# Other PSUM banks for a transposed output, and work moved between slots, in a hybrid SGU and GLA block

## The chip, the cores and the metric

One core of one Trainium2 chip runs the whole layer as a single launch. TensorE (PE) multiplies, VectorE (DVE), ScalarE (ACT) and GpSimd (POOL) do the rest, and SyncE (SP) issues the DMAs. The metric is device time in microseconds, from runs of the whole program; lower is better. All numbers of the profile come from one execution, taken by the hardware profiler.

## The reference, cut to what matters

The layer takes x, 512 tokens of 1024 channels in float32, and computes

```
p   = x @ W_in + b_in        # u, v | q, k, vg, r, low-rank gate | g_A, g_B
y_A = gelu(u) * (W_s layernorm(gelu(v)) + b_s)   # per 128-token chunk, 8 groups, W_s lower triangular
y_B = rmsnorm(gla(q, k, vg, gate)) * gn * silu(r)   # 4 heads, decay per key channel
m   = sigmoid(g_A) * y_A + sigmoid(g_B) * y_B
h   = layernorm(alpha * x + m @ W_out)
out = layernorm(alpha * h + relu(h @ W_1)^2 @ W_2)   # inner width 4096
```

The gated linear attention (gla) is causal: token t sees token s at or before it with the weight q_t k_s exp(sum of the log gates between them), summed over 128 key channels of a head.

## The kernel before, in words

**Products.** Every large product is made three times: both operands are split into a high half (a cast on ScalarE, L90) and a low half (a subtraction on VectorE, L91), and high x high, high x low and low x high are added up in one PSUM bank. A group is 24 matmuls (8 slices of the inner dimension, three passes) into one bank. The four banks of `ps_m` take the groups in turn; `ps_a` has two more single banks (tag `aux`) for everything small; `ps_s` holds one tile of two banks for the attention scores (tag `sc`).

**Weights.** They come as 146 chunks of 128x1024, in the order that `_stream` (L1019) writes out. `load_to` (L102) issues a chunk's DMA on SP into a raw buffer, `split_to` (L127) makes its two halves in the next of the seven buffers of `wpool`, so chunk i + 7 is split as soon as PE is done with chunk i. The last matrix product needs eight chunks at once; the eighth, the very last, is put aside into a part of `xh` and `xl` that is free by then (L135).

**Slots.** `pump` (L183) runs behind each group of the first part and gives out, in the order in which they were planned, the small jobs that `at` has put on that slot. The groups are: V in slots 0 to 7 (L634), U in 8 to 15 (L649), Q and K of the second head pair in 16 to 19 (L674), the values VG in 20 to 27 (L697), g_A in 28 to 35 (L704), then r, r, g_B, g_B four times from slot 36 on (L734, L769).

**Scores.** For each of two pairs of heads, `plan_pair` (L530) takes a list of 20 steps, counted from slot 0 for the first pair and from 16 for the second: the gates; for each of three levels a difference (`level_diff`), the exponent and products (`level_prep`) and the scores of the two heads (`level_score`, L474); the diagonal (`diag_prep`, `diag_score`) of the two heads; the part between chunks (`inter`); two transposes (`kd_turn`, L393). The exponents of the keys, `kt`, have one buffer, so a level's `kt` waits for the scores of the level before. The scores' tile has one buffer too. `chunk_out` (L499) makes one chunk's output of one head in an `aux` bank, from slot 29 on for the first pair and 35 on for the second.

**The gating unit.** `mix` (L652) multiplies one channel group by its W_s into an `aux` bank, and VectorE reads it (L658) and multiplies it into u (L666). Two of them stand in the hand-over of each Q or K group of slots 16 to 19 (L678).

**Branches.** `r_take` (L709) transposes the normalised output of the attention into an `aux` bank, `yt`, and multiplies it with silu(r) (L714).

**The order of the engines.** PE runs in the order in which the program is written. The other engines' order is set by a planner that works with its own costs, up to line 803; from there on (the two layers of width 4096) ScalarE, VectorE and GpSimd run in program order too.

**The two layers.** The inner width is cut into four blocks of 1024. For three of them the second layer is done with seven products in place of eight (Strassen's scheme): `seven_products` (L879) yields the products P0 to P6, in the order `ORDER`, each with two chunks of weights (some of them sums or differences of two loaded chunks, L124) and an operand that is made one product ahead (`operand`, L847: a difference L824, a high half, a low half). Between them lie eight pieces j0 to j7 of the first layer for the next block, each a group with one chunk (`block`, L834): j0 P0 j1 P1 ... j5 P5 j6 j7 P6. The chunks in the stream stand in the same order. After P4 and P5 of the last block, `together` (L905) adds partial results up on VectorE, three and four operations. Then both halves of the last block are split in parts (`in_parts`, L942: `Fs` behind P5, `xh` and `xl` ahead of P6), and the last matrix product (L972 on) runs over eight chunks: four with `Fs`, four with `xh`.

Of the kernel before, what the change touches and what calls it, by code (L numbers as in the profile page):

```python
# [8 lines left out]
F32 = mybir.dt.float32  # L9
# [6 lines left out]
P = 128  # L16
# [4 lines left out]
KT = D // P  # L21
DK = 128
DV = 256
NCH = T // P
# [25 lines left out]
def hybrid_block(  # L50
# [23 lines left out]
    def pool(stack, name, **kw):  # L74
        kw.setdefault("bufs", 1)
        return stack.enter_context(tc.tile_pool(name=name, reuse_waits="tile", **kw))
# [9 lines left out]
    ps_s = pool(ctx, "ps_s", bufs=1, space=PSUM)  # L86
    ps_a = pool(ctx, "ps_a", bufs=2, space=PSUM)
# [6 lines left out]
    NB = DF // 512  # L94
    STREAM = _stream()
    NCHUNK = len(STREAM)

    raws, chunks, kept = {}, {}, {}
    lanes, ring = {0: rpool}, {lane: [] for lane in LANES}
# [2 lines left out]
    def load_to(n):  # L102
        while state["load"] < min(n, NCHUNK):
            i = state["load"]
            kind, lane, key, news = STREAM[i]
            if news is not None:
                ends = ring[lane]
                if len(ends) >= LANES[lane] and ends[-LANES[lane]] >= state["split"]:
                    break
                raw = lanes[lane].tile([P, 1024], F32, name=f"raw{i}", tag="raw")  # L110
                nc.sync.dma_start(raw, w_all[news])
                kept.setdefault(key, []).append(raw)
                users = [j for j in range(i + 1, NCHUNK) if STREAM[j][2] == key]
                users = [j for n_, j in enumerate(users) if all(STREAM[x][3] is None for x in users[:n_])]
                ends.append(max([i] + (users if key else [])))
            raws[i] = kept[key][-1:] if kind == "one" else kept[key][-2:]
            state["load"] = i + 1

    def sum_to(n):
        while state["sum"] < min(n, state["load"]):  # L120
            i = state["sum"]
            raw, *other = raws[i]
            if other:
                nc.vector.tensor_tensor(raw, raw, other[0], op=ALU.add if STREAM[i][0] == "sum" else ALU.subtract)  # L124
            state["sum"] = i + 1

    def split_to(n):  # L127
        while state["split"] < min(n, NCHUNK):
            i = state["split"]
            load_to(i + 1)  # L130
            if i < NCHUNK - 1:
                hi = wpool.tile([P, 1024], F32R, name=f"wh{i}", tag="wh")
                lo = wpool.tile([P, 1024], F32R, name=f"wl{i}", tag="wl")
            else:
                hi, lo = (a[:, 4:6, :].rearrange("p k t -> p (k t)") for a in (xh, xl))  # L135
            sum_to(i + 2)
            raw = raws[i][0]
            if i:
                split(hi, lo, raw)
            chunks[i] = (hi, lo)  # L140
            state["split"] = i + 1
        load_to(n + sum(LANES.values()) if 1 in lanes else n + RAW_BUFS)
# [381 lines left out]
    pr0 = pair_new(0, gp0)  # L524
# [5 lines left out]
    def plan_pair(pr, n0, steps):  # L530

        at(n0 + steps[0], lambda: gates(pr))
        for lv in range(3):
            d_, p_, s0, s1 = steps[1 + 4 * lv : 5 + 4 * lv]
            at(n0 + d_, lambda lv=lv: level_diff(pr, lv))
            at(n0 + p_, lambda lv=lv: level_prep(pr, lv))
            at(n0 + s0, lambda lv=lv: level_score(pr, lv, 0))
            at(n0 + s1, lambda lv=lv: level_score(pr, lv, 1))
        p0, p1, s0, s1, i_, k0, k1 = steps[13:]
        for j, (p_, s_) in enumerate(((p0, s0), (p1, s1))):  # L540
            at(n0 + p_, lambda j=j: diag_prep(pr, j))
            at(n0 + s_, lambda j=j: diag_score(pr, j))
        at(n0 + i_, lambda: inter(pr))
        at(n0 + k0, lambda: kd_turn(pr, 0))
        at(n0 + k1, lambda: kd_turn(pr, 1))

    S_V, S_U, S_QK = 0, 8, 16
    S_VG, S_GA = 20, 28
    S_R, S_O = 36, 52
    plan_pair(pr0, 0, (1, 3, 3, 5, 6, 7, 7, 8, 10, 11, 11, 12, 13, 13, 14, 14, 16, 16, 17, 18))  # L550


    def ln_apply(dst, src, st, g, b, tmpp, tag, parts=1):
# [57 lines left out]
    def col_job(name, take):  # L611
        u0 = take_chunks(1)
        col_group(xh, xl, u0, name, slice(0, T), take)
        pump()
        split_to(u0 + 1 + W_BUFS)
# [4 lines left out]
    def u_take(e):  # L620
        return lambda ps: nc.scalar.activation(AT_[:, e, :], ps, AF.Gelu_apprx_tanh, bias=col("u", e))
# [24 lines left out]

    at(S_U + 1, mix_bias)

    for e in range(KT):  # L649
        col_job(f"u{e}", u_take(e))  # L650

    def mix(g):  # L652
        gs = slice(g * P, (g + 1) * P)
        pm = ps_a.tile([P, NCH, P], F32, name=f"pm{g}", tag="aux")
        for c in range(NCH):
            nc.tensor.matmul(pm[:, c, :], bufB[:, c, gs], wst[:, g, :], start=True, stop=True)
        tm = temp(f"mx{g}")
        nc.vector.scalar_tensor_tensor(  # L658
            tm.rearrange("p (c s) -> p c s", s=P),
            pm,  # L660
            col("sgg", g),
            mixb[:, gs].unsqueeze(1).broadcast_to([P, NCH, P]),
            op0=ALU.mult,
            op1=ALU.add,
        )
        nc.vector.tensor_mul(AT_[:, g, :], AT_[:, g, :], tm)  # L666


    pr1 = Pair()
    pr1.hp = 1  # L670
    pr1.q = gt.tile([P, 2, T], F32, name="q1", tag="q")
    pr1.k = gt.tile([P, 2, T], F32, name="k1", tag="k")
    plan_pair(pr1, S_QK, (2, 4, 5, 6, 7, 7, 8, 9, 10, 10, 10, 12, 13, 13, 15, 15, 16, 16, 17, 18))
    for e in range(4):  # L674

        def take(ps, e=e):
            qk_take(pr1, e, ps)
            mix(2 * e)  # L678
            mix(2 * e + 1)

        col_job(f"qk1_{e}", take)
    sgu.close()
# [24 lines left out]

    def r_take(e, t1):
        def f(ps):  # L709
            pt = ps_a.tile([P, NCH, P], F32, name=f"yt{e}", tag="aux")  # L710
            for c in range(NCH):
                nc.tensor.transpose(pt[:, c, :], bufB[:, c, e * P : (e + 1) * P], ident)
            nc.scalar.activation(t1, ps, AF.Silu, bias=col("r", e))
            nc.vector.scalar_tensor_tensor(  # L714
                t1.rearrange("p (c s) -> p c s", s=P),
                pt,
                col("gn", e),
                t1.rearrange("p (c s) -> p c s", s=P),
                op0=ALU.mult,
                op1=ALU.mult,  # L720
            )

        return f
# [203 lines left out]
    for p in range(PAIRS - 1):  # L927
        F_ = fp.tile([P, 2, 4, T], F32, name=f"F{p + 1}", tag="F")
        jobs = block(take_raw(F_, 0)) + block(take_raw(F_, 1))
        for n, product in enumerate(seven_products(F, p, F_)):  # L930
            jobs[n]()
            if n == 6:
                jobs[7]()
            product()
        F = F_

# [2 lines left out]
    jobs = block(take_raw(F_, 0)) + block(take_raw(F_, 1))  # L939
# [6 lines left out]
        return hi, lo  # L946

    for n, product in enumerate(seven_products(F, PAIRS - 1, None)):
        jobs[n]()
        if n == 6:  # L950
            jobs[7]()
            parts.append(in_parts(1, hh[:, 0:4, :], hl[:, 0:4, :]))
        product()
        if ORDER[n] == 4:
            together(7, ((1, 4),))
            together(4, ((1, 2),), (1, 0))
        if ORDER[n] == 1:
            together(6, ((1, 1), (-1, 2), (1, 3)))
            together(7, ((1, 1),))
        if n == 5:  # L960
            Fs = fp.tile([P, 2, 4, T], F32R, name="Fs", tag="F")
            parts.append(in_parts(0, Fs[:, 0], Fs[:, 1]))
    split_to(NCHUNK)
    together(7, ((-1, 5),))
# [54 lines left out]
def _stream():  # L1019

    n = 16 * 4
    out = [("one", 0, None, c) for c in range(n)]
    f1 = n
    f2 = n + 4 * (DF // 512)
    f1_jobs = iter(range(f1, f2))
    take = lambda k: [("one", 0, None, next(f1_jobs)) for _ in range(k)]

    def operand(p, m, h):  # L1030
        b = lambda i, j: f2 + 8 * p + 2 * (2 * (i - 1) + j - 1) + h
        kind, c = {
            2: ("one", b(1, 1)),
            6: ("sum", b(1, 2)),
            3: ("sum", b(2, 2)),
            5: ("one", None),
            7: ("sum", b(2, 1)),
            4: ("sum", b(1, 1)),
            1: ("less", b(2, 2)),
        }[m]  # L1040
        return (kind, h, (p, h), c)

    out += take(8)
    for p in range(PAIRS):
        products = [[operand(p, m, h) for h in range(2)] for m in ORDER]
        for i, product in enumerate(products):
            out += take(1 + (i == 6)) + product
    out += [("one", 0, None, f2 + 8 * PAIRS + c) for c in range(8 * (DF // 1024 - PAIRS))]
    return out

# [73 lines left out]
```

## Time and profile before

| | |
|---|---|
| median of 3 runs | 780.04 us (779.6 to 780.37) |
| the profiled execution | 780.24 us, its span 778.3 us |
| PE | 758.2 us busy, 97% |
| VectorE | 489.9 us, 63% |
| ScalarE | 355.5 us, 46% |
| GpSimd | 67.3 us, 9% |
| HBM traffic | 82.48 MB read, 2.10 MB written |

In the rows of the profile the first number of a timeline row is the start, the second the duration, both in us; [2.14 <-DVE qt L437] is idle time of the engine just before and what ended it. A row of the waits has the total, the number of times and the longest. A row of the chain has start, duration, engine, tile, line and how many instructions are merged. A matmul's end is modelled, so neighbours overlap in the rows.

### The profile page before, as it was taken

Reading aid. Unit: us, or ns where it says so; the run is one execution under the profiler, and the core shown is the slowest. Engines: PE = TensorE matmul, PEld = TensorE weight load, DVE = VectorE, ACT = ScalarE, POOL = GpSimd, SP = SyncE. Lnnn points to the kernel's source line nnn. Section 1 sums busy time; section 2 is a strip of 40 time slices with the busy share of each in tenths; the row PEclk is TensorE's granted clock in tenths of the full one; section 3 lists DMA queues with packets and bytes.
Section 4 is the critical chain, followed back from the end, with each engine's and each line's share of the span. In section 5 each row is a group of like instructions: output and inputs, shape, how many; then the busy total and the mean of one; then the engine's idle time right before and its main releaser. Section 6 shows DMA issues by size and latency. Waiting matters only on the chain.

```text
span 778.3 us, 8853 instructions
## 1 busy us (share of the span) xinstructions
PE 758.2 (97%) x3498; PEld 629.6 (81%) x3498; DVE 489.9 (63%) x584; ACT 355.5 (46%) x453; POOL 67.3 (9%) x87
## 2 busy tenths in 40 slices
PE   9998999989999989999999999999999999999996
PEld 7887888877888877888888987888888888888785
DVE  6569756668666532445447545774687568769955
ACT  5476864354146444454322444555554445454300
POOL 1015400013202211000001000000000000000011
PEclk9999999999999999999999999999999999999999
DMA  8723332200341231422232422444144424335111
GB/s 275 267 79 105 111 120 81 82 28 28 108 136 55 101 116 32 135 92 88 101 99 78 163 82 83 160 136 136 56 161 136 149 69 151 128 126 163 54 55 54
DMA packets 25609, 85.15 MB, mean 109 GB/s; under 512 B 3104, under 2 KB 3360, under 8 KB 25568
## 3 DMA queue, kind: packets, MB, share of 16 engines
q1 hardware_dynamic: 25568, 84.59, 33.1%
q8 instruction: 27, 0.44, 0.2%
q14 instruction: 14, 0.11, 0.1%
HBM read 82.48 MB, written 2.10 MB: 109 GB/s over the span
## 4 chain that ended last, share of the span: by engine, by line
PE 85%; DVE 6%; ACT 3%; issue 2%; POOL 1%; DMA 1%; SPq 0%; DVEq 0%; POOLq 0%; ACTq 0%
PE f L608 22%; PE m L898 14%; PE ps L204 12%; PE r L608 6%; PE gb L608 6%; PE u L608 6%; PE f L984 5%; PE ga L608 4%; PE first L271 2%; PE qk L608 2%; PE sc L478 2%; DVE wl L91 2%; DMA raw<-in_w_all 1%; POOL qt L419 1%; ACT wh L90 1%
## 5 line engine op out<-in xcount | busy, mean ns | idle before, releaser
L91 DVE TENSOR_TENSOR wl<-raw,wh 128x1024 fp32r<-128x1024 f32 x144 | 176.6, 1236 | 154.5 <-ACT wh L90 147.7
L90 ACT CAST wh<-raw 128x1024 fp32r<-128x1024 f32 x144 | 148.6, 1044 | 139.0 <-PE ps L204 34.0
L608 PE MATMUL f<-xh,wl 128*128 128x512 f32 (+1 forms) x288 | 105.5, 366 | 0.0
L608 PE MATMUL f<-xh,wh 128*128 128x512 f32 (+1 forms) x288 | 105.4, 366 | 0.0
L608 PE MATMUL f<-xl,wh 128*128 128x512 f32 (+1 forms) x288 | 105.4, 366 | 0.0
L898 PE MATMUL m<-wh,ol 128*128 128x512 f32 x168 | 66.5, 396 | 0.5 <-DVE ol L91 0.5
L898 PE MATMUL m<-wh,oh 128*128 128x512 f32 x168 | 66.6, 396 | 0.3 <-ACT oh L90 0.3
L898 PE MATMUL m<-wl,oh 128*128 128x512 f32 x168 | 66.3, 395 | 0.0
L608 PEld LDWEIGHTS f<-xl,wh 128*128 128x128 f32 x288 | 54.3, 189 | 9.0
L608 PEld LDWEIGHTS f<-xh,wh 128*128 128x128 f32 x288 | 54.3, 189 | 8.9
L608 PEld LDWEIGHTS f<-xh,wl 128*128 128x128 f32 x288 | 54.3, 189 | 8.8
L204 PE MATMUL ps<-wh,xh 128*128 128x512 f32 x128 | 51.1, 399 | 0.0
L204 PE MATMUL ps<-wl,xh 128*128 128x512 f32 x128 | 50.1, 391 | 0.0
L204 PE MATMUL ps<-wh,xl 128*128 128x512 f32 x128 | 50.0, 390 | 0.0
L827 ACT ACTIVATE F<-f 128x512 f32<-128x512 f32 (+1 forms) x28 | 15.0, 536 | 75.5 <-PE f L608 75.5
L124 DVE TENSOR_TENSOR raw<-raw,raw 128x1024 f32<-128x1024 f32 x30 | 36.6, 1221 | 7.3 <-DMA raw<-in_w_all 7.0
L419 POOL TENSOR_TENSOR qt<-cum 128x768 f32<-128x768 f32 (+2 forms) x18 | 30.3, 1713 | 115.5 <-DVE cum L374 102.2
L898 PEld LDWEIGHTS m<-wh,ol 128*128 128x128 f32 x168 | 31.6, 188 | 8.4 <-DVE ol L91 1.0
L898 PEld LDWEIGHTS m<-wh,oh 128*128 128x128 f32 x168 | 31.6, 188 | 7.9 <-ACT oh L90 0.7
L898 PEld LDWEIGHTS m<-wl,oh 128*128 128x128 f32 x168 | 31.7, 189 | 7.3
L991 POOL TENSOR_TENSOR rs_l<-rs_l,nhalf 128x1 f32<-128x1 f32 x4 | 3.9, 987 | 334.1 <-DVE rs_l L990 334.1
L90 ACT CAST oh<-d 128x1024 fp32r<-128x1024 f32 x15 | 15.7, 1048 | 37.4 <-DVE d L824 37.4
(226 smaller groups left out, 1523.7 us busy)
## 6 DMA issues: line engine op xcount, KB each, us to landing
raw<-in_w_all SPq DMA_DIRECT2D x139, 512.0 KB, 3.3
xr<-in_x SPq DMA_DIRECT2D x8, 256.0 KB, 4.0
out<-bufA SPq DMA_DIRECT2D x8, 256.0 KB, 2.0
bufA<-in_xT SPq DMA_DIRECT2D x3, 512.0 KB, 8.5
brow<-in_b_in SPq DMA_DIRECT2D x4, 256.0 KB, 5.9
g<-in_ln_g SPq DMA_DIRECT2D x2, 512.0 KB, 4.8
b<-in_ln_b SPq DMA_DIRECT2D x2, 512.0 KB, 6.0
bufA<-in_xT SPq DMA_DIRECT2D x2, 256.0 KB, 3.4
```

Source lines behind the costliest of these rows:

```text
L90: nc.scalar.copy(hi, src)
L91: nc.vector.tensor_tensor(lo, src, hi.bitcast(F32), op=ALU.subtract)
L124: nc.vector.tensor_tensor(raw, raw, other[0], op=ALU.add if STREAM[i][0] == "sum" else ALU.subtract)
L204: nc.tensor.matmul(ps, s_, m_, start=(k == 0 and i == 0), stop=(k == KT - 1 and i == 2))
L271: nc.tensor.matmul(first[e], s_, m_[:, k, :], start=(k == 0 and i == 0), stop=(k == KT - 1 and i == 2))
L419: getattr(nc, DIFF_Q).tensor_tensor(qv[:, :, s0 : s0 + n, :], c4[:, :, d:4, :], c4[:, :, 0:n, h - 1 : h].broadcast_to([P, na, n, h]), op=A ...
L478: nc.tensor.matmul(sc[:, c, 0:192], pr.kt[:, jc * P : (jc + 1) * P], pr.qt[:, jc, :], start=True, stop=True)
L608: nc.tensor.matmul(ps, s_, m_, start=(k == 0 and i == 0), stop=(k == KT - 1 and i == 2))
L827: nc.scalar.activation(dst, ps, AF.Relu)
L898: nc.tensor.matmul(ps, s_, m_, start=(k == 0 and i == 0), stop=(k == 3 and i == 2))
L984: nc.tensor.matmul(ps, s_, m_, start=(f == 0 and i == 0), stop=(f == 7 and i == 2))
L991: nc.gpsimd.tensor_tensor(rs, rs, nhalf, op=ALU.pow)
```

## The change

Four edits:

- `r_take` transposes into one bank of the scores' tile (`ps_s`, tag `sc`) and no longer into an `aux` bank.
- The eight mixes leave the hand-over of the Q and K groups; they stand one per slot in slots 12 to 19.
- In both step lists the first level's scores come one slot later, and most of what follows moves with them. In the second pair the first head's diagonal products come one slot later as well, with its scores where they were; in the first pair the diagonal's two scores stand in slots 15 and 16, before in 14 and 16.
- Each block's pieces and products go j0 j1 P0 j2 P1 ... j7 P6, in the program and in the stream of chunks. The chunk put aside is the third last and no longer the last; the two behind it are split into the buffers of `wpool`.

```
@@ in the program's setup, and split_to
+    ASIDE = NCHUNK - 3
     def split_to(n):
+        n += n > ASIDE
         while state["split"] < min(n, NCHUNK):
...
-            if i < NCHUNK - 1:
+            if i != ASIDE:
@@ the step lists
-    plan_pair(pr0, 0, (1, 3, 3, 5, 6, 7, 7, 8, 10, 11, 11, 12, 13, 13, 14, 14, 16, 16, 17, 18))
+    plan_pair(pr0, 0, (1, 3, 3, 6, 7, 7, 7, 9, 11, 11, 11, 13, 14, 14, 15, 15, 16, 16, 17, 18))
...
-    plan_pair(pr1, S_QK, (2, 4, 5, 6, 7, 7, 8, 9, 10, 10, 10, 12, 13, 13, 15, 15, 16, 16, 17, 18))
+    plan_pair(pr1, S_QK, (2, 4, 5, 7, 8, 8, 8, 10, 11, 11, 11, 13, 14, 14, 15, 15, 16, 16, 17, 18))
@@ the mixes (the loop over u moves behind mix)
+    for g in range(KT):
+        at(S_QK - 4 + g, lambda g=g: mix(g))
+    for e in range(KT):
+        col_job(f"u{e}", u_take(e))
...
             qk_take(pr1, e, ps)
-            mix(2 * e)
-            mix(2 * e + 1)
@@ r_take
-            pt = ps_a.tile([P, NCH, P], F32, name=f"yt{e}", tag="aux")
+            pt = ps_s.tile([P, 2, NCH, P], F32, name=f"yt{e}", tag="sc")[:, 0]
@@ the blocks, both loops
-        jobs[n]()
-        if n == 6:
-            jobs[7]()
+        if n == 0:
+            jobs[0]()
+        jobs[n + 1]()
@@ _stream
-            out += take(1 + (i == 6)) + product
+            out += take(1 + (i == 0)) + product
```

More of the change, by code (lines that the diff above doesn't have):

```diff
@@ L647, in hybrid_block @@
     at(S_U + 1, mix_bias)
-    for e in range(KT):
-        col_job(f"u{e}", u_take(e))
     def mix(g):
@@ L948, in hybrid_block @@
     for n, product in enumerate(seven_products(F, PAIRS - 1, None)):
-        jobs[n]()
+        if n == 0:
+            jobs[0]()
+        jobs[n + 1]()
         if n == 6:
-            jobs[7]()
             parts.append(in_parts(1, hh[:, 0:4, :], hl[:, 0:4, :]))
```

## Prediction

> **What bounds the kernel now.** I read the page first, then the waits of PE, the granted clock in windows, the chain of waits, and last the order of instructions around each stall.
>
> ```profile
> span 778.3 us, 8853 instructions
> PE 758.2 (97%) x3498; PEld 629.6 (81%) x3498; DVE 489.9 (63%) x584; ACT 355.5 (46%) x453; POOL 67.3 (9%) x87
> ```
>
> PE is busy for 97% of the span. The change leaves out no matmul, so it can win only the time in which PE stands still or runs slowly. Where that is, the waits of PE say (total, times, longest):
>
> ```profile
> PE po L504 <- DVE t L714: 3.1, 2, 2.0
> PE sc L478 <- DVE qt L437: 2.9, 2, 2.1
> PE pt L396 <- DVE mx L658: 2.1, 2, 1.0
> PE pz L364 <- DVE KD L397: 1.3, 1, 1.3
> ...
> PE f L984 <- DVE xl L91: 0.8, 1, 0.8
> PE m L898 <- DVE ol L91: 0.5, 1, 0.5
> PE m L898 <- ACT oh L90: 0.3, 1, 0.3
> PE po L504 <- ACT bufB L522: 0.3, 1, 0.3
> ```
>
> The rows shown sum to 11.3 us. Two things come on top. The longest stalls cost clock too (window, its length, busy time of PE, PEld, DVE, ACT, POOL, then PEclk):
>
> ```profile
> 66.00:72.00 6.00, 3.86 (x12) 3.52 (x12) 5.28 (x8) 3.90 (x4) 1.77 (x3) 0.72 0.09 12
> 286.00:292.00 6.00, 3.95 (x15) 3.02 (x14) 2.85 (x4) 3.38 (x7) 0.74 (x2) 0.86 0.27 89
> 292.00:298.00 6.00, 6.00 (x26) 4.80 (x25) 0.00 (x0) 0.99 (x4) 0.74 (x2) 0.85 0.00 0
> ```
>
> At 66 us 28% of 6 us is lost, 1.7 us; from 286 us 14% and 15%, again 1.7 us. And idle time is counted short. The chain has the two kinds of group, a second-layer product and a first-layer piece, and the timeline has one stall:
>
> ```profile
> 692.70 5.59 PE m L898 x24
> 698.28 5.46 PE f L608 x24
> ```
>
> ```profile
> 730.49 0.40 PE L984 MATMUL f<-xh 128*128 128x512 f32 x1
> 731.64 0.51 PE L984 MATMUL f<-xl,xh 128*128 128x512 f32 x1 [0.75 <-DVE xl L91]
> ```
>
> Matmuls start every 5.46 / 24 = 0.23 us but are drawn 0.40 long, so one that was due at 730.72 starts at 731.64: 0.92 late where the row says 0.75. I add 0.16 to every stall.
>
> **The change part by part.**
>
> *First scores a slot later, first pair.* A slot is one group.
>
> ```profile
> 68.29 2.73 PE L478 MATMUL sc<-qt,kt 128*128 128x192 f32 x8 [2.14 <-DVE qt L437]
> ```
>
> Level 0's first scores come up at 66.15 and start at 68.29, when VectorE has made their operand. One slot later PE comes to them at 66.15 + 5.46 = 71.6, 3.3 us after the operand is there, so one group covers the wait. Gain: 2.14 + 0.16 + 1.7 of clock = 4.0 us. The later levels move along and keep their distance to the level before, because one kt buffer ties each level to the last one's scores. What is late next is level 1:
>
> ```profile
> 87.33 1.22 DVE L432 TENSOR_TENSOR kt<-kt,k 128x1024 f32<-128x1024 f32 x1 [0.87 <-ACT kt L430]
> 88.98 1.46 PE L478 MATMUL sc<-qt,kt 128*128 128x192 f32 x8
> ```
>
> Its kt is ready 0.43 us before its scores start. It keeps its two groups of distance, but ScalarE and VectorE are ordered by a planner up to line 803 and may be shuffled. No row shows the new order. I bound what it costs over all these slots between a gain of 0.45 (the 0.3 of the bufB row goes too) and a second stall like the first, 4.0, and take 0.8: two thin margins, this one and the first pair's diagonal (whose one group now has a mix's VectorE work beside it), each missed by about 0.4, nearer to the margin seen than to a lost operand.
>
> *Second pair.* The other wait of the L478 row is 2.9 - 2.1 = 0.8; with 0.16 it is 0.9 us, and one VG group covers it. Its diagonal now follows the last level by one group instead of two, but two chunk outputs lie in that gap as well; I cost it at nothing, and if that cover fails it is part of the 0.8 above.
>
> *Mixed groups one per slot.* Before, two mixes stand behind each qk group:
>
> ```profile
> 158.25 1.23 DVE L91 TENSOR_TENSOR wl<-raw,wh 128x1024 fp32r<-128x1024 f32 x1 [4.64 <-ACT wh L90]
> 159.39 1.40 DVE L658 SCALAR_TENSOR_TENSOR mx<-pm,cols_sb,mixb 128x512 f32<-128x512 f32 x2
> ...
> 161.91 0.68 DVE L397 COPY KD<-pt 128x512 f32<-128x512 f32 x1
> ...
> 162.65 0.50 PE L364 MATMUL pz<-a_sb,w2s 128*128 128x512 f32 x1 [1.30 <-DVE KD L397]
> ```
>
> The two mixes take both auxiliary banks, and the transposes behind them wait until VectorE has read the first: 2.1 us in slots 17 and 18, with 2 x 0.16 it is 2.4, and that goes. In slot 18 the order becomes transposes, one mix, two gate products, and a wait stays: the second gate product needs the mix's bank. With only the copy (0.68) and one mx (1.40 / 2 = 0.7) in the way I estimate 0.5; if VectorE takes the weight split (1.23) between them, 0.5 + 1.23 = 1.7. Before, the split runs ahead of mx, so I take 1.5, against the 1.30 + 0.16 now there: nothing won on that half. Net 2.4 us (2.1 to 3.4). The mixes' own work is unchanged, only up to four slots earlier, over groups that hide their VectorE part.
>
> *Turned output in the scores' banks.*
>
> ```profile
> 285.35 0.60 PE L712 MATMUL yt<-ident,bufB 128*128 128x128 f32 x4
> ...
> 288.39 0.75 DVE L714 SCALAR_TENSOR_TENSOR t<-yt,cols_sb,t 128x512 f32<-128x512 f32 x1 [0.39 <-ACT t L713]
> ...
> 289.29 0.67 PE L504 MATMUL po<-bufB,AT 128*128 128x256 f32 x2 [2.05 <-DVE t L714]
> ```
>
> The second chunk output of slot 36 takes the bank that yt holds until 289.1; in slot 37 the same costs the rest of that wait's row, 1.1. With yt in the scores' tile each chunk output reuses a bank of the slot before. That tile has one buffer, but no scores are left by then, and yt is read 3.8 us after it starts while the next yt is at least a group away: nothing to pay. Gain: 2.05 + 0.16 + 1.7, and 1.1 + 0.16: 5.2 us.
>
> *Two first-layer pieces ahead, the start.* The first product waits 0.5 + 0.3 us for its operand; with 2 x 0.16 it is 1.1, and one more piece (5.46) covers it. Gain 1.1. Between the pairs nothing changes for PE: each product's operand is still made one product ahead. The weight loads on SP's queue change places with the pieces:
>
> ```profile
> raw<-in_w_all SPq DMA_DIRECT2D x139, 512.0 KB, 3.3
> ```
>
> A load is issued when its buffer comes free, and by the code at least one step (5.5 us) before its split, as before; 3.3 us to landing fits in that. I cost it at nothing; were one late, its split would be, and seven chunks of depth lie between a split and PE.
>
> *The same, the end.* Here I expect a loss. From line 803 on every engine runs in program order. The last pair went P4 j5 P5 j6 j7 P6 (j a piece, P a product) and then the last matrix product; it becomes j5 P4 j6 P5 j7 P6. VectorE's queue from the piece before P4 on:
>
> ```profile
> 694.96 1.22 DVE L91 TENSOR_TENSOR wl<-raw,wh 128x1024 fp32r<-128x1024 f32 x1 [4.77 <-ACT wh L90]
> ...
> 722.22 2.35 DVE L91 TENSOR_TENSOR wl<-raw,wh 128x1024 fp32r<-128x1024 f32 x2
> ...
> 729.77 0.68 DVE L875 TENSOR_TENSOR acc<-acc,m 128x512 f32<-128x512 f32 x1
> 730.37 1.22 DVE L91 TENSOR_TENSOR xl<-raw,xh 128x1024 fp32r<-128x1024 f32 x1
> ```
>
> The first row waits for j4's end at 692.70. From it VectorE works nearly without a gap (sums, operands, and the halves Fs, xl) to the last chunk's low half at 731.59: 38.9 us after j4's end. PE in that time has three products and three pieces, 33.2 us, and then 22 matmuls of 0.23, 5.0, until it needs that half: 38.2. So VectorE is 0.7 late, which is the 0.75 of the row above. After the change j5 stands where j4 stood, and only j6 and j7 of the pieces are left behind it. VectorE's work shrinks by one split (2.35 / 2) and by one sum that now comes behind the last chunk (0.68): 38.9 - 1.9 = 37.0. PE's shrinks by a whole piece: 38.2 - 5.5 = 32.7. VectorE is 4.3 us late. The piece that moved ahead was VectorE's cover here. Most of it is one wait, at the third-last chunk, whose low half lies two splits (2.35) ahead of the last: due 1.4 us earlier, it is 3.3 late. A stall longer than those that lost 1.7 of clock probably loses clock too, but part of that falls beside the two short waits behind it; I add 0.5 (0 to 1.7). New delay 4.3 + 3 x 0.16 for three waits + 0.5 = 5.3, old 0.9: loss 4.4 us (3.9 to 5.6).
>
> *Sum.* 4.0 + 0.9 + 2.4 + 5.2 + 1.1 - 4.4 - 0.8 = 8.4 us. The profiled execution took 780.24 us, 2 more than its span and 0.2 over the median of the three runs (780.04): 780.04 - 8.4 = **771.6 us**.
>
> [...] The windows above show the clock falling after stalls of 2.14 and 2.05 us. [...] The measurement decides here, and it is 1.7 us each.
>
> **The rivals.**
>
> *The end costs nothing (0.13).* If VectorE's queue were not the limit, for instance because the last chunk's load (its buffer is freed by the split at 722.22) set the 731.64, the 4.4 would not come: 771.6 - 4.4 = 767.2 us. Against it: the row of 730.37 follows its neighbour with no gap.
>
> *A new stall in the planned part (0.18).* The level-1 margin of 0.43 us is lost by a rotated order of ScalarE, with a stall of over 2 us and its clock: 4.0 in place of the 0.8, 771.6 + 3.2 = 774.8 us.
>
> *The slow clock stays (0.06).* If the two slow stretches came by another cause than the stalls, 2 x 1.7 us stays: 775.0 us. [...] Against it: both stretches hold one of the two longest stalls.
>
> *ScalarE's backlog, slower (0.04).* ScalarE is nearly full while the first pair's levels run:
>
> ```profile
> 80.00:100.00 20.00, 20.00 (x89) 16.05 (x88) 12.54 (x19) 18.98 (x18) 8.21 (x10) 1.00 0.39 119
> ```
>
> PE comes to this stretch 4.0 us earlier. If the planner puts level 1's exponent behind that whole backlog, the product on VectorE behind it (1.22) ends at about 101, where the scores want it at 88.98 + 5.46 - 4.0 = 90.4: 10.8 late and 1.7 of clock, in place of the 0.8, so 771.6 - 0.8 + 12.5 = 783.3 us. It ends slower than before once the exponent is more than about 8 us late. Against it: that product starts at 87.33 now, with the same work ahead.
>
> **How the numbers follow.** The forecast has 0.59. The range runs from 767.2, the end at no cost, to 776.0, a new stall (774.8) with 1.2 of the other bounds on top; it leaves out the backlog and the outer halves of the other cases, under 0.2. About 0.2%, 1.6 us, can be told from no change. All cases but the backlog are faster by more: faster 0.93; the backlog gives slower 0.04; 0.03 is left for stalls that eat the whole gain.
>
> **What would show it.** Right: no wait of po on L714, none of pt on mx, no window below full clock near 66 or 289 us, no wait at the first product, and a wait of the last matrix product on VectorE's low halves that grows from 0.8 to about 4. Wrong: that wait small or gone; a wait of sc on kt in slots 9 to 16; a wait on KD or mx over 2 us in slot 18. The forecast fails as a whole if PE's idle time before 330 us stays above 5 us.

## The result, and the profile after

The changed kernel takes 782.87 us (median of 5 runs, 781.62 to 783.33), the kernel before 779.6 beside it (5 runs, 779.16 to 780.37). The ratio is 1.0035, with a 95% interval of 1.0023 to 1.0046. It is 3.3 us slower, where 8.4 us less were forecast. The profiled execution took 782.87 us, its span is 780.8.

The waits of PE in the changed kernel (total, times, longest), whose line numbers are mostly two or three higher than before, so that L480 is the scores' matmul (L478 before) and L987 the last matrix product (L984):

```profile
PE sc L480 <- DVE kt L434: 3.8, 1, 3.8
PE f L987 <- DVE xl L91: 2.8, 1, 2.8
PE sc L480 <- DVE AT L492: 2.1, 1, 2.1
PE pz L366 <- DVE mx L657: 1.3, 1, 1.3
PE wu L240 <- POOL bal L292: 1.1, 1, 1.1
PE pt L398 <- ACT bufB L524: 0.8, 1, 0.8
```

All the waits that were to go have gone: po on L714, the scores on qt, the transposes on mx, the first product on ol and oh. Four have come or grown. Two stand in the first pair: the scores wait 2.1 us for copies out of their own tile (AT) and 3.8 for level 1's kt. One is the last matrix product's, 2.8 in place of 0.8, and one is small (pt on bufB).

The windows around them (length, busy PE, PEld, DVE, ACT, POOL, then PEclk):

```profile
66.00:72.00 6.00, 6.00 (x29) 5.03 (x29) 5.33 (x8) 3.91 (x4) 1.77 (x3) 1.00 0.08 21
78.00:84.00 6.00, 3.88 (x13) 3.37 (x12) 3.16 (x8) 5.17 (x7) 1.04 (x3) 0.72 0.01 3
94.00:100.00 6.00, 2.18 (x8) 1.79 (x7) 3.91 (x7) 5.13 (x6) 0.76 (x1) 0.79 0.26 87
100.00:106.00 6.00, 6.00 (x16) 3.77 (x15) 5.53 (x13) 1.49 (x2) 0.00 (x0) 0.64 0.53 171
286.00:292.00 6.00, 6.00 (x32) 5.12 (x30) 1.62 (x2) 3.98 (x7) 1.29 (x3) 1.00 0.12 48
726.00:732.00 6.00, 3.03 (x7) 1.93 (x8) 6.00 (x9) 1.05 (x1) 0.00 (x0) 0.75 0.26 89
732.00:738.00 6.00, 6.00 (x20) 4.72 (x19) 5.90 (x7) 0.00 (x0) 0.00 (x0) 0.68 0.00 0
```

The two old holes, at 66 and 286 us, are at full clock with PE full. In their place are three holes, each with a low clock in it or behind it. By the clock's records the granted clock was 0.50 for 3.413 us from 80.44, 6.827 from 97.51 and 6.827 from 728.97: of these 17.1 us PE had work in 14.8 (its waits end at 80.53, 98.43 and 730.21), so 7.4 are lost. Before it was twice 3.413, all of it at work, 3.4 lost.

The stages put it in place. The first group of U starts at 82.97 (83.53 before), the first transpose behind the branches at 415.00 (416.51), the last matrix product at 722.77 (725.65), and PE's last matmul ends at 773.86 (771.37). So up to U 0.6 is won where 4.0 was forecast; from there to the transpose 0.9, where 8.5 less a part of the 0.8 was; the blocks win 1.4, forecast 1.1; and the last product loses 5.4, forecast 4.4. The sum is the 2.5 us by which the span is longer.

**The first pair.** VectorE in the changed kernel (start, duration, idle time ahead of it and what ended it):

```profile
75.64 1.22 DVE L385 TENSOR_TENSOR QI<-QI,q 128x1024 f32<-128x1024 f32 x1 [0.86 <-ACT QI L384]
77.59 0.69 DVE L590 BATCH_NORM_STATS2 sgst<-bufB 128x6 f32<-128x512 f32 x1 [0.72 <-ACT bufB L589]
...
79.00 1.38 DVE L492 COPY_PREDICATED AT<-masks,sc 128x384 f32<-128x384 uint32 x3
83.09 0.69 DVE L590 BATCH_NORM_STATS2 sgst<-bufB 128x6 f32<-128x512 f32 x1 [2.71 <-ACT bufB L589]
...
84.02 2.36 DVE L91 TENSOR_TENSOR wl<-raw,wh 128x1024 fp32r<-128x1024 f32 x2
86.30 0.68 DVE L587 TENSOR_TENSOR vt<-ps,brow 128x512 f32<-128x512 f32 x1
89.44 1.49 DVE L91 TENSOR_TENSOR wl<-raw,wh 128x1024 fp32r<-128x1024 f32 x1 [2.46 <-ACT wh L90]
90.85 0.68 DVE L590 BATCH_NORM_STATS2 sgst<-bufB 128x6 f32<-128x512 f32 x1
...
92.04 1.16 DVE L411 TENSOR_TENSOR kt<-cum 128x1024 f32<-128x1024 f32 x1
...
97.06 1.23 DVE L434 TENSOR_TENSOR kt<-kt,k 128x1024 f32<-128x1024 f32 x1 [0.39 <-ACT kt L432]
```

and in the kernel before:

```profile
73.11 0.68 DVE L585 TENSOR_TENSOR vt<-ps,brow 128x512 f32<-128x512 f32 x1
73.72 0.59 DVE L490 COPY_PREDICATED AT<-masks,sc 128x384 f32<-128x384 uint32 x1
...
79.42 1.21 DVE L409 TENSOR_TENSOR kt<-cum 128x1024 f32<-128x1024 f32 x1
```

Level 0's first scores do what the prediction said: they start at 71.5, and nothing waits. But the copies that read them, at 73.72 before, now run at 79.00. Nothing that they read is late: they stand behind the QI product and behind one more row of V, its statistics (L590, which wait for ScalarE's gelu) and its addition (L587). PE wants the same tile for the second head at 78.4 and gets it at 80.53. Then the whole of level 1 goes the same way. Its difference (L411), which was at 79.42, runs at 92.04, behind two more rows of V with their idle times. ScalarE shows what those idle times wait for:

```profile
79.87 1.24 ACT L575 ACTIVATE bufB<-bufB,rs_sg 128x1024 f32<-128x1024 f32 x1 [0.79 <-POOL rs_sg L574]
81.13 1.28 ACT L589 ACT_TABLE_LOAD   x1
82.42 0.63 ACT L589 ACTIVATE bufB<-vt 128x512 f32<-128x512 f32 x1
...
87.22 1.25 ACT L575 ACTIVATE bufB<-bufB,rs_sg 128x1024 f32<-128x1024 f32 x1 [2.28 <-POOL rs_sg L574]
...
94.84 1.24 ACT L575 ACTIVATE bufB<-bufB,rs_sg 128x1024 f32<-128x1024 f32 x1 [1.15 <-POOL rs_sg L574]
95.98 1.04 ACT L432 ACTIVATE kt<-kt 128x1024 f32<-128x1024 f32 x1
```

Each row of V is a ring through three engines: VectorE's statistics, GpSimd's small steps, ScalarE's normalisation (L575), and behind it on ScalarE the next row's gelu, for which VectorE's next statistics wait. Three times ScalarE waits there for GpSimd. Level 1's exponent (L432) has the third of these normalisations ahead of it. The scores, due at 94.61, start at 98.43.

**The end.** VectorE in the last product of the changed kernel:

```profile
717.59 2.48 DVE L910 TENSOR_TENSOR bufB<-bufB,acc 128x1024 f32<-128x1024 f32 x2
720.10 1.23 DVE L910 TENSOR_TENSOR bufB<-bufB 128x1024 f32<-128x1024 f32 x1
721.25 1.22 DVE L910 TENSOR_TENSOR bufB<-bufB,acc 128x1024 f32<-128x1024 f32 x1
722.38 2.49 DVE L91 TENSOR_TENSOR Fs<-Flast,Fs 128x512 fp32r<-128x512 f32 x4
...
728.93 1.22 DVE L91 TENSOR_TENSOR xl<-raw,xh 128x1024 fp32r<-128x1024 f32 x1
730.06 2.36 DVE L91 TENSOR_TENSOR wl<-raw,wh 128x1024 fp32r<-128x1024 f32 x2
```

It works without a gap, and the third-last chunk's low half (the first xl<-raw row) ends at 730.15, where PE has waited since 727.40. This is the queue that the prediction walked through.

### The profile page after: what moved, and what is told of

Same layout as the page of the kernel before. It is cut to its first block, busy times and chain, and to the rows that moved or that the text cites. A ratio compares the mean times of both kernels' runs of the same rounds, so it can differ in the third digit from the quotient of the medians.

```text
span 780.8 us, 8845 instructions
## 1 busy us (share of the span) xinstructions
PE 760.4 (97%) x3498; PEld 631.5 (81%) x3498; DVE 490.4 (63%) x584; ACT 351.8 (45%) x449; POOL 67.6 (9%) x87
## 4 chain that ended last, share of the span: by engine, by line
PE 82%; DVE 8%; ACT 4%; issue 2%; POOL 2%; DMA 1%; SPq 0%; DVEq 0%; ACTq 0%; POOLq 0%
PE f L610 21%; PE m L900 13%; PE ps L206 13%; PE gb L610 6%; PE r L610 6%; PE f L987 6%; PE u L610 4%; PE ga L610 3%; PE qk L610 3%; DVE wl L91 2%; PE first L273 2%; PE sc L480 2%; DMA raw<-in_w_all 1%; PE pm L655 1%; DVE bufB L910 1%
```

## The experiments

The theory after this result: both losses are order in VectorE's queue. In the first pair the planner put work that was ready (copies, level 1's difference) behind work that waits for the ring of row norms; at the end four sums stand ahead of the halves. The rivals: the first pair is late by its own chain (table loads, exponents, products), whatever the order; and the losses are made by several edits together. The first four runs and one later one do one edit alone.

**The first pair's list alone.**

```
-    plan_pair(pr0, 0, (1, 3, 3, 5, 6, 7, 7, 8, 10, 11, 11, 12, 13, 13, 14, 14, 16, 16, 17, 18))
+    plan_pair(pr0, 0, (1, 3, 3, 6, 7, 7, 7, 9, 11, 11, 11, 13, 14, 14, 15, 15, 16, 16, 17, 18))
```

> The kernel before with the first pair's new step list alone. Theory (queue order): the stall of 2.1 us at 66 us goes with its clock (4.0 us), but level 0's copies and level 1's difference fall behind the last V groups in VectorE's queue, where they wait for ScalarE; two stalls of about 2.1 and 3.8 us near 78 and 94 us with 5.1 us of clock come in, so some 7 us slower, 786 to 788. Rival (the mixes did it: their place ahead of the Q and K groups shuffled the planner's order): no stall near 78 or 94, 4 us faster, about 776.

It took 784.33 us beside 779.47, ratio 1.0071 [1.0043, 1.0098]: 4.9 us slower from one line. PE's waits in it:

```profile
PE sc L478 <- DVE kt L432: 5.5, 1, 5.5
...
PE sc L478 <- DVE AT L490: 2.1, 1, 2.1
```

Both new stalls come from this list alone. VectorE's order there is the changed kernel's, and the product on kt starts at 96.70, there at 97.06. The longer stall is 5.5 and not 3.8 because PE comes to it 2.0 us earlier (at 92.60, there at 94.61): behind the 2.1 the clock did not fall here, where the changed kernel lost 1.7. Behind the 5.5 it fell for 6.827 us.

**The turned output alone.**

```
-            pt = ps_a.tile([P, NCH, P], F32, name=f"yt{e}", tag="aux")
+            pt = ps_s.tile([P, 2, NCH, P], F32, name=f"yt{e}", tag="sc")[:, 0]
```

> The kernel before with only the transposed output in the scores' banks. Theory: both waits of po on L714 go and the slow clock near 290 us with them, 5.2 us faster, about 774.5. Rival (the chunk outputs then wait for ScalarE and GpSimd to free the bank of the slot before): half of it or less, 777 or more, with po waiting on bufB L522.

775.76 beside 779.47, ratio 0.9952 [0.9937, 0.9966]: 3.7 us won, not 5.2. Both waits on L714 are gone, 3.1 of idle time; the clock that was to come back with them did so only in part. In this profile the 2.12 us wait at 67 us cost no clock, but three short waits of 1.05, 1.05 and 1.30 us around 150 to 163 us, which cost none before, are followed by 3.413 us at half clock.

**The mixes alone.**

```
+    for g in range(KT):
+        at(S_QK - 4 + g, lambda g=g: mix(g))
...
-            mix(2 * e)
-            mix(2 * e + 1)
```

> The kernel before with only the mixes one per slot. Theory: the waits of pt on mx go (2.4 us), the one of pz stays near 1.3, nothing new near 78 or 94 us, 2 to 2.5 us faster, about 777.5. Rival (the mixes' place shuffles ScalarE and VectorE in slots 7 to 9): stalls near 78 and 94 us, slower than before.

775.91 beside 779.47, ratio 0.9954 [0.9939, 0.9969]: 3.6 us won, more than the 2.4 of idle time. The waits of 2.12 and 2.05 us are still in its profile, at 67 and 284 us, and no half clock is behind either.

**The order of pieces alone** (in the stream, as shown, and in both loops, with the chunk put aside).

```
-            out += take(1 + (i == 6)) + product
+            out += take(1 + (i == 0)) + product
```

> The kernel before with only the new order of pieces and products and the new chunk aside. Theory: 1.1 to 1.3 us won at the first product, 5.4 us lost in the last matrix product on VectorE's low halves and the clock behind it, so 4 us slower, about 783.7. Rival (the end stall in the changed kernel came from the half-clock phase of that run alone): under 1 us slower or faster.

783.88 beside 779.47, ratio 1.0062 [1.0044, 1.0079]: 4.4 us slower. The waits on ol and oh are gone, the one on xl is 2.8.

**The same with the sums late.** To move VectorE's cover rather than take it away, the four sums after P5 are issued behind the last chunk's split.

```
         product()
...
-        if ORDER[n] == 1:
-            together(6, ((1, 1), (-1, 2), (1, 3)))
-            together(7, ((1, 1),))
...
+    together(6, ((1, 1), (-1, 2), (1, 3)))
+    together(7, ((1, 1),))
```

> The new order of pieces and products as in e4_ffn, but the four sums that VectorE makes behind the last block's P5 (4.9 us) are issued behind the last chunk's split. Theory (VectorE's queue is what the last product waits for, 4.3 us late): the low halves come 4.9 us sooner, the stall of 2.8 us and its clock go, and the 1.1 to 1.3 us of the first product stay: 1.5 to 2 us faster than before, about 778. Rival (the last chunks' loads or ScalarE's casts set the stall): the stall keeps 2 us or more, 782 or more.

776.73 beside 779.62, ratio 0.9967 [0.9955, 0.9979]. No matmul of the last product waits for VectorE, and it is 7.2 us under the kernel without the move. It is 1.3 us faster than was expected (778), and where these come from is not shown. VectorE's queue there:

```profile
721.59 2.50 DVE L91 TENSOR_TENSOR xl<-Flast,xh 128x512 fp32r<-128x512 f32 x4
723.99 0.69 DVE L877 TENSOR_TENSOR acc<-acc,m 128x512 f32<-128x512 f32 x1
724.59 1.22 DVE L91 TENSOR_TENSOR xl<-raw,xh 128x1024 fp32r<-128x1024 f32 x1
725.73 2.36 DVE L91 TENSOR_TENSOR wl<-raw,wh 128x1024 fp32r<-128x1024 f32 x2
...
728.59 2.49 DVE L910 TENSOR_TENSOR bufB<-bufB,acc 128x1024 f32<-128x1024 f32 x2
```

The half that ended at 730.15, 7.4 us after the last product began, now ends at 725.81, 2.5 after (it begins at 723.34), with the sums behind it, over matmuls that don't need them. The order of pieces is a gain once its loss at the end is paid.

**The change with the first pair's old list.**

```
-    plan_pair(pr0, 0, (1, 3, 3, 6, 7, 7, 7, 9, 11, 11, 11, 13, 14, 14, 15, 15, 16, 16, 17, 18))
+    plan_pair(pr0, 0, (1, 3, 3, 5, 6, 7, 7, 8, 10, 11, 11, 12, 13, 13, 14, 14, 16, 16, 17, 18))
```

> The changed kernel with the first pair's old step list, all else as changed. Theory: the stalls near 78 and 94 us go (9 us with their clock), the 2.1 us at 66 us comes back with small ones behind it; the gains of the transposed output (3.7), the mixes (3.6) and the second pair's list (0.9) remain, the order at the end costs 4.4: about 776. Rival (the stalls come from the sum of the edits in the planned part): stalls near 78 and 94 remain, 780 or more.

776.2 beside 779.62, ratio 0.996 [0.9945, 0.9975]. The stalls at 78 and 94 us are gone, and the old one at 67 is back with its clock; 6.7 us less than the whole change. The list, not its company, makes the two stalls, and without it the change is 3.4 us faster than the kernel before.

**The first pair's list, with the order held.** This one takes the planner's order away and keeps the list. In V's second half the slot's jobs are planned ahead of the row's own work; the row's addition, gelu and statistics are held behind the last copy, difference and exponent issued; rows 2 and 3 are normalised together in slot 7; and level 2's exponent of qt stands behind level 1's of kt.

```
-            consume(t, ps)
-            pump()
+            if early:
+                pump()
+            with behind() if early else ExitStack():
+                consume(t, ps)
+            if not early:
+                pump()
...
-            if half:
-                row = bufB[:, t, :]
+            for i in ((), (0,), (1,), (), (2, 3))[t + 1 if half else 0]:
+                row = bufB[:, i, :]
```

> The kernel before with the first pair's new list as in e1_list0, and the issue order held by hand around the last V groups: level 0's copies ahead of the sum of the same slot, level 1's difference and exponent ahead of slot 7's V work, the last two rows' normalisation and level 2's exponent behind them. Same work, only its place in the two queues. Theory (queue order): the stall of 5.5 us near 92 goes to under 1.5, the one of 2.1 near 78 to about 1.2; with the stall at 66 gone the kernel is 1 to 3.5 us faster than before, 776 to 779. Rival (ScalarE or VectorE is simply full there): the two stalls together keep 5 us or more, slower than before.

777.61 beside 779.62, ratio 0.998 [0.9965, 0.9996]: 6.7 us under the same list in the planner's order, and 2.0 under the kernel before.

```profile
PE sc L492 <- DVE AT L504: 1.5, 1, 1.5
...
PE sc L492 <- DVE kt L446: 1.3, 1, 1.3
```

The two stalls are 2.8 us together instead of 7.6, and no clock is lost. No arithmetic was taken away, so it was the order. But even so the slot later is worth 2.0 and not the 4.0 of the forecast.

**Without V's gelu**, on the kernel with the first pair's new list alone. What makes the ring late, the table that ScalarE loads for the gelu (1.28 us, at 81.13 in the changed kernel), or GpSimd's steps?

```
-            nc.scalar.activation(dst, tm, AF.Gelu_apprx_tanh)
+            nc.scalar.activation(dst, tm, AF.Identity)
```

> The kernel before with the first pair's new list, as in the first of these runs (784.3; stalls of 2.1 and 5.5 us), with the gelu on v left out: a plain copy with bias stands in its place on ScalarE, so no table is loaded for it; output differs in that. Theory A (VectorE waits in its queue for ScalarE's gelu, late because of table loads): both stalls fall under 1 us each. Theory B (the planner's order itself, with GpSimd's chain of row norms, is what is late, the gelu only rides along): the 5.5-us stall stays over 3 us.

780.81 us in one run. The copies' stall stays, 2.5 us; the one on kt is gone. ScalarE ahead of the copies:

```profile
74.52 1.25 ACT L573 ACTIVATE bufB<-bufB,rs_sg 128x1024 f32<-128x1024 f32 x1 [2.96 <-POOL rs_sg L572]
75.67 0.61 ACT L587 ACTIVATE bufB<-vt 128x512 f32<-128x512 f32 x1
78.60 1.24 ACT L573 ACTIVATE bufB<-bufB,rs_sg 128x1024 f32<-128x1024 f32 x1 [2.32 <-POOL rs_sg L572]
79.75 0.61 ACT L587 ACTIVATE bufB<-vt 128x512 f32<-128x512 f32 x1
```

No table load is left between 70 and 82 us and ScalarE idles, yet each row's activation (75.67, 79.75) stands behind a normalisation that waits 2 to 3 us for GpSimd, and VectorE's statistics and copies stand behind the activation. GpSimd's three steps take only 1.2 us there (77.33 to 78.57); it waited itself 2.85 us for VectorE's statistics, so the wait is that of the whole ring. So for the first stall the loads are not the cause (theory A falls). But theory B's sign, a second stall over 3 us, did not come either. For the second the run decides nothing, since the planner gave it another order: level 1's exponent came ahead of the normalisation and not behind it.

**The second pair's list alone.**

```
-    plan_pair(pr1, S_QK, (2, 4, 5, 6, 7, 7, 8, 9, 10, 10, 10, 12, 13, 13, 15, 15, 16, 16, 17, 18))
+    plan_pair(pr1, S_QK, (2, 4, 5, 7, 8, 8, 8, 10, 11, 11, 11, 13, 14, 14, 15, 15, 16, 16, 17, 18))
```

> The kernel before with the second pair's new step list alone. The prediction's term: 0.9 us less (the 0.8-us wait of the scores on qt is gone). Rival: a wait of the transposes on bufB near 265 us (0.8 in the changed kernel) takes its place, and the time stays within 0.5 us.

779.88 beside 779.85, ratio 0.9991 [0.9977, 1.0006]. The rival was right: the 0.8 on qt is gone and the same length has come at 267 us.

```profile
PE pt L396 <- ACT bufB L522: 0.8, 1, 0.8
```

**Three kernels put together.** The first has the old list for the first pair, the other edits, and the old order of pieces in the last block only (in the stream, as shown, and in its loop):

```
+            out += take(1 + (i == (0 if p < PAIRS - 1 else 6))) + product
```

> The first pair's old list, the new one of the second pair, the mixes one per slot, the transposed output in the scores' banks; two pieces ahead in the first two blocks, the last block in the old order with the new chunk aside. Theory: 3.7 + 3.6 + 0.9 + 1.2 and 0.5 at the last product, so 770 us. Rival (a piece less behind P5 at the block borders costs elsewhere): a wait of m in the blocks, 773 or more.

770.45 beside 779.62, ratio 0.9887 [0.987, 0.9903].

The second has the old list, the other edits as they are, and the late sums; the third has the new list with its order held as well:

```
+    together(6, ((1, 1), (-1, 2), (1, 3)))
+    together(7, ((1, 1),))
```

> All edits but the first pair's new list, with the late sums and no issue order held by hand. Theory: 776.2 - 7.2 = 769.0, the 2.1-us wait at 66 us still there, none in the last product. Rival (the new order of pieces is worth nothing or costs something else at its start): no better than the version with the old order in the last block, 770.5 or more.

> All four edits with both mends: the first pair's new step list with the issue order held by hand (score copies ahead of the V addition of their slot, level 1's difference and exponent ahead of slot 7's V work, the last two row normalisations and level 2's exponent behind it), and the four sums of P5 behind the last chunk's split. Theory (the two losses are queue order in VectorE and ScalarE, one in each place, and independent): all edits with the old list took 776.2; less 7.2 for the late sums is 769.0; the 66-us wait and its clock (up to 4.0) go and 1.5 + 1.3 of the two short stalls stay, so 767 to 769. Rival (the gains of the parts overlap, one wait taking another's place): 771 or more.

770.19 and 769.5 beside 779.85, ratios 0.9871 [0.9853, 0.9889] and 0.9862 [0.984, 0.9883]. They are 1.2 and at least 0.5 us over what was expected, and the intervals of the three don't part them. All three are faster than the kernel before and the changed one. The rival of the second (no better than 770.5) is not excluded: a new order in the last block with late sums is worth what the old order there is, within a microsecond.

## Why the prediction was wrong, step by step

The edits measured alone, beside the terms of the sum:

| step | forecast | alone |
|---|---|---|
| first pair, a slot later | -4.0, and a part of +0.8 | +4.9 |
| second pair | -0.9 | 0.0 |
| mixes | -2.4 | -3.6 |
| turned output | -5.2 | -3.7 |
| pieces ahead, start and end | -1.1 + 4.4 = +3.3 | +4.4 |
| sum | -8.4 | +2.0 |

The whole change measures +3.3, so the parts nearly add up, and one row makes 8 of the 10 us between forecast and sum.

**The step that failed** is the one that reads: "The later levels move along and keep their distance to the level before", with its allowance, "I bound what it costs over all these slots between a gain of 0.45 ... and a second stall like the first, 4.0, and take 0.8". Two groups do still lie between level 0's last scores, which free kt, and level 1's first (slots 7 and 9, before 6 and 8). But level 1's difference and exponent kept slot 7 in the list: the scores that they wait for stood one slot ahead of them, and stand in the same slot now. The order in the queues came out anew, with them behind V's rows. In the changed kernel's profile the two new stalls cost 2.12 + 3.82, twice 0.16, and 1.7 + 3.0 of clock (half of the 3.32 and 5.91 us at half speed in which PE had work): 10.9 us, against 0.8. Even the upper bound of 4.0 was too low, for it was set by a stall that the profile already had. A bound by place would have been wide enough: the ready instruction put behind all that waits beside it. The prediction did have such a bound, as the rival that ends slower, but for ScalarE alone, with 0.04, and only level 1 was looked at. The copies, which hold the scores' single tile, were not asked after: "What is late next" was also the second head's scores, one group later.

**The rivals.** "A new stall in the planned part" named the mechanism, and the row that would show it, a wait of sc on kt in slots 9 to 16, came; its price was one stall of 4.0. "ScalarE's backlog, slower" came out in its sign and nearly in its time (783.3), and the product on kt is 3.8 us late, not 10.8; the copies' stall makes up part of the rest. That the times lie so close is luck: its sum has 8.5 us for the first pair (12.5 - 4.0), and the list alone cost 4.9. And the longer part lies in VectorE's queue: the difference starts at 92.04, 8.6 us after the scores that free kt end (83.43), while ScalarE's exponent follows the difference (to 93.20) by 2.8.

**Turned output and mixes** were right in every wait that goes and stays (pz keeps 1.29, forecast 1.5). Their sizes differ by the clock: 1.7 per long stall was taken as certain. "The measurement decides here, and it is 1.7 us each" was drawn from two stalls of one execution, and the fourteen profiles have nineteen such stalls with five low clocks behind them (below). The 1.4 us in which the turned output falls short fits this term: its four runs have a mean granted clock of 0.995 or 0.996, as have 29 of the 36 runs of the kernel before beside the experiments, so next to no clock was won. The profiled execution that the prediction read had 0.993, more clock lost than in most.

**Second pair.** "One VG group covers it" was right for the wait, but another of 0.84 us has come later on, at 269 us. It is small, and what orders ScalarE's step behind it was not tried.

**The blocks** won 1.4 (forecast 1.1). **The end** was right: VectorE's queue is the limit, the longest wait is at the third-last chunk, and the stage loses 5.4 (forecast 4.4, bounds 3.9 to 5.6). The parts differ: 2.81 of waiting there instead of 3.3, about 0.75 in the three matmuls just ahead of it and nearly none behind it, and 6.827 us at half clock, 5.59 of them with PE at work, so 2.8 lost instead of 0.5. Less waiting and more lost clock nearly make up for each other, so that the loss lies within its bounds is in part luck. In the order of pieces alone, where the half clock lasted 3.413, the stage loses 4.2.

## What to carry to other kernels

Where a planner or scheduler orders the engines, moving a step by one slot moves what stands ahead of it in each queue: list what is ready early and ask which waiting instruction it may now stand behind, above all where a single buffer hangs on it, and bound the cost by that queue, not by the longest stall seen. When work moves ahead on the busiest engine, look for the engine whose backlog it was covering; here losing the cover cost 4 to 5 us at the end, and moving four sums behind it gave back 7. In the changed kernel every wait that was to go was gone, while behind the stalls of 2.05 to 2.15 us the clock was low in 5 cases of 19: count such a clock by its average, not by its worst.

## What the runs showed of the hardware

**The clock.** Apart from the stretch at the very end of each run, the half-clock stretches in the fourteen profiles last 3.413 or 6.827 us, nothing between. Behind stalls of 2.05 to 2.15 us there was one in 5 of 19 cases; behind stalls of 2.45 us and more in 6 of 6. The same three short waits (1.05, 1.05, 1.30 around 160 us) had one behind them in 5 of 8 kernels. The same stall at 67 us has one in the kernel before (2.14 us) and none with the turned output alone (2.12), which changes nothing before 285 us. So the length of a stall alone does not tell whether clock is lost behind it. All clock records of a profile begin on one grid of 3.413 us (80.44, 97.51 and 728.97 in the changed kernel are 5 and 185 steps apart, 68.47 and 290.34 in the kernel before are 65). Of the nineteen stalls, the five that lost clock lay with at least 2.04 us inside one step of that grid, and the half clock began with the next step (in the kernel before the stall ends at 68.29 and the clock is 0.50 from 68.47); the fourteen that lost none lay with at most 1.97 in one. The grid lies differently to the kernel's start from profile to profile: 68.47 is 0.2 us behind a multiple of 3.413, 80.44 is 1.9. The place in the grid parts the five from the fourteen; that it is the cause was not tried.

**GpSimd beside VectorE.** The small steps of the row norms in the changed kernel, first beside VectorE's addition and copies of 78.44 to 80.38, then beside its two subtractions wl<-raw,wh of 84.02 to 86.38:

```profile
78.61 0.21 POOL L169 TENSOR_SCALAR rs_sg<-mv_sg 128x1 f32<-128x1 f32 x1 [5.23 <-DVE mv_sg L572]
78.91 0.56 POOL L172 TENSOR_TENSOR rs_sg<-rs_sg,nhalf 128x1 f32<-128x1 f32 x1
...
84.11 1.22 POOL L169 TENSOR_SCALAR rs_sg<-mv_sg 128x1 f32<-128x1 f32 x1 [4.27 <-DVE mv_sg L572]
85.41 1.40 POOL L172 TENSOR_TENSOR rs_sg<-rs_sg,nhalf 128x1 f32<-128x1 f32 x1
```

A step on one element per partition takes 1.22 us instead of 0.21, and the next 1.40 instead of 0.56. The first of them also takes 1.08 us in the kernel before at 85.24, beside such a subtraction (85.07 to 86.24), and 1.09 in the changed kernel at 92.20, beside level 1's difference (92.04 to 93.20). The two excesses, 1.01 and 0.84, lengthen the ring by some 1.8 us at 84 us; no run took VectorE's work there away, so that it is the cause is argued from the overlap and not shown, and so is the part in the stalls.
